# Transposing by two 64-row halves into a pair of neighbouring PSUM banks, in a two-layer decoder trunk

## The chip, the cores and the metric

The kernel runs on one core of one Trainium2 chip. The metric is the device time of one execution in microseconds. Three executions of the kernel before took 1024.15, 1024.07 and 1023.37 us; the median is 1024.07.

The core has several engines that run their own instruction queues side by side and wait for each other by semaphores: PE (TensorE) multiplies matrices, ACT (ScalarE) applies functions and copies, DVE (VectorE) does elementwise arithmetic, POOL (GpSimd) does a little here, and SP (SyncE) issues the DMAs that bring the weights. PE's results land in PSUM, which the kernel uses as 8 banks of 128 partitions by 512 f32; ACT and DVE read them from there.

## The reference

Two layers of a decoder block on 256 tokens of width 1024, in f32:

```python
def hybrid_layer(h, ...):
    h = h + 0.5 * swiglu(rms_norm(h, ffn1_norm), ffn1_w_gate, ffn1_w_up, ffn1_w_down)
    u = rms_norm(h, mix_norm)
    proj = u @ w_in
    # 8 heads of stick-breaking attention (width 512) and 4 heads of latent attention
    # (width 512); each group normalised, concatenated, one output projection
    h = h + mixed @ w_out
    h = h + 0.5 * swiglu(rms_norm(h, ffn2_norm), ffn2_w_gate, ffn2_w_up, ffn2_w_down)
    gate = jax.nn.sigmoid(rms_norm(h, ple_norm) @ w_ple_gate)
    h = h + gate * (p_i @ w_ple_proj)
    return h

def swiglu(x, w_gate, w_up, w_down):
    return (jax.nn.silu(x @ w_gate) * (x @ w_up)) @ w_down
```

After the two layers stands a last `rms_norm`. The hidden width of the FFNs is 2816. Every matrix product sums over the axis that must lie on the 128 partitions, so activations that come out with tokens on the partitions are transposed before the next product.

## The kernel before

**Tiling.** The 256 tokens are two halves t = 0 and 1 of 128. `h` holds the residual stream with tokens on the partitions, 1024 columns for each t. An operand of a matrix product is held transposed, in 8 chunks c of 128 features by 256 tokens, and as two f32r parts, high and low (`x..h` and `x..l`). `mm3` computes a product in three passes: high by high, high by low, low by high (lines 217, 218 and 219 of the profile, in any order of the parts). A pass of 512 columns is one PE instruction.

**Weights.** `Unit.load` fetches 128 × 1024 f32 into `raw` (6 buffers). ACT rounds it to `wh` (L132), DVE subtracts to get `wl` (L133). There are 6 buffers of each. The down projections of the second and third FFN blocks use a seven-product scheme (`Seven`, L168 to L174).

**Transpositions.** PE transposes 128 × 128 tiles by a product with an identity (`ident`, in `c_sb`) into a PSUM bank. There are four kinds. `turn_h` (L328) transposes `h` between stages, four chunks at a time, so two banks for one token half; the tiles are named `xt_a` (FFN1 to mixer), `xt_mix` (mixer to FFN2), `xt_b` (FFN2 to the embedding stage) and `xt_e` (that stage to the next layer). After it, `split` brings each 128 × 128 tile to the next operand: ACT copies it times a gain to the high part (L262), DVE takes the low part from tile and high part (L263). `Gates.add` (L445) transposes the product `pr` of gate and up, four tiles for one t, into a tile `ft`. `turned` (L735) transposes the normalised attention outputs into `yt`. `mla_turn` (L813) transposes the softmax numerators into `pt`.

**PSUM.** One pool `ps` of 8 banks with one tag, so any tile takes the next bank that comes free. A tile that finds none waits until the readers of the oldest are done.

**Order.** The kernel is written once in program order; a scheduler then lists the instructions of each engine by when it thinks their operands are ready, keeping the manual order constraints set by `after`. Work that should come a little later than it becomes possible is put in by `soon(us, f)`: `f` is emitted when PE has been given so many more microseconds of products by the kernel's own count (`tick`: 0.68 for an `mm3` of 512 columns, 0.36 for 256 or fewer). `flush` emits what is left. `residual`, called when a token half's down projection is complete, adds to `h` (L354), asks for the two `turn_h` at 1.2 and 1.9 and then sums squares for the norm (`junk`, L298). `lagging` runs the last chunks of a down projection for t = 0 ahead of those for t = 1, so that t = 0's transposition and splits run beside t = 1's products; the first products of the next stage on t = 0 then run beside those of t = 1.

Of the kernel before, what the change touches and what calls it, by code (L numbers as in the profile page):

```python
# [17 lines left out]
P = 128  # L18
# [27 lines left out]
def trunk(ctx: ExitStack, tc: tile.TileContext, xT, xr, pT, w, gains, fgain, consts, out):  # L46
# [9 lines left out]
    ps = pool("ps", 8, space=PSUM)  # L56

    def bank(name):
        return ps.tile([P, 512], F32, tag="A", name=name)

# [196 lines left out]
    def split(x, src, c, gcol, name, ts=slice(0, T)):  # L257

        xh, xl = x
        g = g_sb[:, gcol : gcol + 1]  # L260
        return (
            nc.scalar.activation(xh[:, c, ts], src, AF.Copy, scale=g),  # L262
            nc.vector.scalar_tensor_tensor(xl[:, c, ts], src, g, xh[:, c, ts].bitcast(F32), op0=ALU.mult, op1=ALU.subtract),  # L263
        )
# [57 lines left out]
    def turn_h(x, t, n, gcol, name):  # L322

        a = bank(f"xt{t}{n}_{name}")
        behind = newest_mm[0]
        for j in range(4):
            c = 4 * n + j
            after(nc.tensor.transpose(a[:, j * P : (j + 1) * P], h[:, t, c * P : (c + 1) * P], ident), behind)  # L328
# [21 lines left out]
    def residual(x, n, d, t, scale, tag, gcol, wait=(1.2, 1.9)):  # L350

        for f in range(2):
            c = half(f)
            nc.vector.scalar_tensor_tensor(h[:, t, c], d[t][f], scale, h[:, t, c], op0=ALU.mult, op1=ALU.add)  # L354
# [30 lines left out]
    class Gates:  # L385
# [19 lines left out]
        def sums(self, i):  # L405
# [6 lines left out]
            s1, s2, s3, s4 = (two[k // 2][:, k % 2].rearrange("p (a b) -> p a b", a=2) for k in range(4))  # L412
# [23 lines left out]
        def add(self, i, t, pr, more):  # L436
# [4 lines left out]
            def go():  # L441
                a = bank(f"ft_{self.tag}_{i}{t}")[:, : n * P]
                behind = newest_mm[0]
                for j in range(n):
                    after(nc.tensor.transpose(a[:, j * P : (j + 1) * P], pr[:, j * P : (j + 1) * P], ident), behind)  # L445
                a = a.rearrange("p (a b) -> p a b", a=n)

                ks = slice(2 if i in SEVEN and t else 0, n)
                fh, fl = both(f, slice(None), ks, slice(t * P, (t + 1) * P))
                nc.scalar.activation(fh, a[:, ks], AF.Copy)  # L450
                nc.vector.tensor_tensor(fl, a[:, ks], fh.bitcast(F32), ALU.subtract)
                self.turned[i, t] = a
                if i in SEVEN and t:
                    self.sums(i)

            soon(1.3 + 0.9 * t + more, go)
# [8 lines left out]
    def ffn(x, n, tag, gcol, between=None, feed=None):  # L465
        gates = Gates(tag)

        def gated(i, t, g, u, m=512):
            s = flat("w0", f"s_{tag}_{i}{t}")[:, :m]
            silu = nc.scalar.activation(s, g, AF.Silu, scale=n.col(t))  # L470

            def rest(more=0.0):
                pr = flat("w1", f"pr_{tag}_{i}{t}")[:, :m]
                nc.vector.scalar_tensor_tensor(pr, u, n.col(t), s, op0=ALU.mult, op1=ALU.mult)
                gates.add(i, t, pr, more)
# [3 lines left out]
        for i in range(NBLK):  # L479
# [4 lines left out]
            if last:  # L484
# [3 lines left out]
                for t in range(2):  # L488
                    silu, rest = gated(i, t, g[t][:, 0:T], g[t][:, T : 2 * T], T)
                    rest()  # L490
# [14 lines left out]
            else:  # L505
# [8 lines left out]
                if i == 1 and feed:  # L514
                    load_consts()
                    exp = newest[0]
                    for t in range(2):
                        silu, r = gated(0, t, first[0][t], first[1][t])
                        after(silu, exp)
                        r(4.5)  # L520
                rests = [gated(i, t, g[t], u[t])[1] for t in range(2)]
# [3 lines left out]
            for r in rests:  # L525
                r()
# [18 lines left out]
        p.update((i, bank(f"p{i}_{tag}")) for i in (1, 5, 6, 7))  # L545
# [27 lines left out]
    def mix(x, n, L, g0):  # L573
# [18 lines left out]
        def sb_scores(hp):  # L592

            st[hp] = zs = [bank(f"z{L}_{hp}_{e}") for e in range(2)]
# [44 lines left out]
        va = [bank(f"v{L}_{t}") for t in range(2)]  # L639
# [18 lines left out]
        uv = wide([Unit(4, again=u) for u in uv])  # L658
        tok_mm(va[1], uv, x, 1)
# [17 lines left out]
        ov = [bank(f"ov{L}_{t}") for t in range(2)]  # L677
# [50 lines left out]
        def turned(o, c0, gcol, name, parts=(0, 1)):  # L728

            for i in parts:  # L730
                a = pair(f"yt{i}_{name}")
                for j in range(2):
                    c = 2 * i + j
                    for t in range(2):
                        nc.tensor.transpose(a[:, j, t * P : (t + 1) * P], o[t][:, c * P : (c + 1) * P], ident)  # L735
                for j in range(2):
                    c = 2 * i + j
                    split(y, a[:, j], c0 + c, gcol + c, name)
# [28 lines left out]
        for i in range(2):  # L767
# [4 lines left out]
            nc.vector.tensor_tensor(kn[:, 2 * i : 2 * i + 2], a, bc(rkv, 2), ALU.mult)  # L772
        ckvT = column(rkv, f"kv{L}")
# [33 lines left out]
        def mla_turn(hp):  # L807
            ex = st["p", hp]
            st["t", hp] = pt = wt("w2", f"pt{L}{hp}", 2, W)
# [281 lines left out]
```

## Time and profile before

| what | before |
|---|---|
| median of three executions | 1024.07 us |
| profiled execution | 1024.05 us |
| its span | 1022.1 us |
| granted TensorE clock | 0.997 |
| DVE busy | 713.2 us, of which wl (L133) 381.8 |
| ACT busy | 603.8 us, of which wh (L132) 332.3 |
| SP's loads of raw | 338 of 512 KB, 16 of 256 KB |

The span runs from the first to the last instruction of one profiled execution; the execution's own time lies 1.95 us above it. A line of the order of time reads: start in us, duration in us, engine, source line, operation, what it writes and reads, shape, number of instructions merged, and where the engine had been idle, for how long and what released it. PEld is the load of stationary operands, which overlaps the products. PE's matmuls are pipelined, so a duration is longer than the distance to the next start, and the distance is what a matmul costs. A row of a group of instructions (`x16 | 5.3, 365 | ...`) gives the number, busy time in all, mean duration in ns and the idle time before. Where durations of one line are listed, they are the least, the median and the greatest.

### The profile page before, as it was taken

What the parts mean: (1) busy time and instruction counts of PE and PEld (TensorE: products, weight loads), DVE (VectorE), ACT (ScalarE), POOL (GpSimd) and SP (SyncE); (2) the same over time, 40 slices, a digit from 0 to 9 for tenths busy, and PEclk for the clock granted to TensorE, in tenths of its full rate; (3) what the DMA queues carried; (4) which work ended last, traced back from release to release, by engine and by line L of the source; (5) the groups of instructions that cost most, each with busy time, mean ns of one, the idle gap of its engine ahead of it and who ended that gap; (6) DMA issues with size and microseconds to landing.
All of it is one profiled execution on the core that took longest, in us unless ns stands there. A gap on an engine that the chain in (4) does not pass through costs nothing.

```text
span 1022.1 us, 13726 instructions
## 1 busy us (share of the span) xinstructions
PE 1010.7 (99%) x5130; PEld 854.9 (84%) x5130; DVE 713.2 (70%) x991; ACT 603.8 (59%) x918; POOL 11.3 (1%) x13
## 2 busy tenths in 40 slices
PE   9999999999999999999999999999999999999996
PEld 8788888899888888888888888889998888888885
DVE  5766579766776665788765656888676756657975
ACT  5755465667565554565764545557766745546664
POOL 0000000100100000000000000001010000000000
PEclk9999999999999999999999999999999999999998
DMA  8865546664246555366565555486623465553651
GB/s 281 317 232 189 180 135 222 216 208 157 83 143 207 186 185 186 123 208 235 183 210 184 185 185 165 145 265 206 207 85 124 154 215 186 186 187 132 220 173 42
DMA packets 53490, 187.39 MB, mean 183 GB/s; under 512 B 6064, under 2 KB 6192, under 8 KB 53424
## 3 DMA queue, kind: packets, MB, share of 16 engines
q1 hardware_dynamic: 52992, 185.95, 54.1%
q8 instruction: 40, 0.66, 0.3%
q10 hardware_dynamic: 432, 0.57, 0.2%
q14 instruction: 26, 0.21, 0.1%
HBM read 185.45 MB, written 1.05 MB: 182 GB/s over the span
## 4 chain that ended last, share of the span: by engine, by line
PE 93%; ACT 3%; DMA 2%; DVE 1%; issue 1%; SPq 0%; DVEq 0%; ACTq 0%
PE g_b L219 4%; PE g_b L217 4%; PE g_b L218 4%; PE g_a L219 4%; PE g_a L217 4%; PE g_a L218 4%; PE u_b L218 4%; PE u_b L217 4%; PE u_b L219 4%; PE u_a L218 3%; PE u_a L219 3%; PE u_a L217 3%; PE d_b L217 3%; PE d_b L219 3%; PE d_b L218 3%; PE d_a L219 3%
## 5 line engine op out<-in xcount | busy, mean ns | idle before, releaser
L133 DVE TENSOR_TENSOR wl<-raw,wh 128x1024 fp32r<-128x1024 f32 (+1 forms) x322 | 381.8, 1195 | 203.6 <-ACT wh L132 199.3
L132 ACT ACTIVATE wh<-raw 128x1024 fp32r<-128x1024 f32 (+1 forms) x322 | 332.3, 1039 | 239.7 <-PE u_b L219 50.2
L173 ACT ACTIVATE wh<-raw 128x1024 fp32r<-128x1024 f32 x56 | 59.5, 1062 | 48.5 <-PE d_b L219 13.3
L174 DVE TENSOR_TENSOR wl<-raw,wh 128x1024 fp32r<-128x1024 f32 x56 | 67.4, 1220 | 18.5 <-ACT wh L173 17.4
L217 PE MATMUL d_a<-wh,fh_a 128*128 128x512 f32 x128 | 50.3, 394 | 0.0
L217 PE MATMUL d_b<-wh,fh_b 128*128 128x512 f32 x128 | 50.3, 393 | 0.0
L218 PE MATMUL d_a<-wl,fh_a 128*128 128x512 f32 x128 | 50.0, 391 | 0.0
L218 PE MATMUL d_b<-wl,fh_b 128*128 128x512 f32 x128 | 50.0, 391 | 0.0
L219 PE MATMUL d_b<-wh,fl_b 128*128 128x512 f32 x128 | 49.9, 389 | 0.0
L219 PE MATMUL d_a<-wh,fl_a 128*128 128x512 f32 x128 | 49.9, 389 | 0.0
L168 DVE TENSOR_TENSOR raw<-raw,raw 128x1024 f32<-128x1024 f32 x32 | 38.7, 1219 | 8.1 <-DMA raw<-in_w 8.0
L217 PE MATMUL g_b<-wh,x_mix0h 128*128 128x512 f32 x96 | 38.4, 400 | 0.0
L217 PE MATMUL g_b<-wh,x_mix1h 128*128 128x512 f32 x96 | 38.4, 400 | 0.0
L217 PE MATMUL g_a<-wh,x0h 128*128 128x512 f32 x96 | 38.1, 399 | 0.3 <-ACT x0h L262 0.3
L217 PE MATMUL g_a<-wh,xe0h 128*128 128x512 f32 x96 | 38.4, 400 | 0.0
L219 PE MATMUL g_a<-wh,xe0l 128*128 128x512 f32 x96 | 37.6, 391 | 0.0
L219 PE MATMUL g_b<-wh,x_mix1l 128*128 128x512 f32 x96 | 37.5, 390 | 0.0
L219 PE MATMUL g_b<-wh,x_mix0l 128*128 128x512 f32 x96 | 37.5, 390 | 0.0
L218 PE MATMUL g_b<-wl,x_mix0h 128*128 128x512 f32 x96 | 37.4, 390 | 0.0
L218 PE MATMUL g_b<-wl,x_mix1h 128*128 128x512 f32 x96 | 37.4, 390 | 0.0
L218 PE MATMUL g_a<-wl,xe0h 128*128 128x512 f32 x96 | 37.4, 390 | 0.0
L219 PE MATMUL g_a<-wh,x0l 128*128 128x512 f32 x96 | 37.3, 390 | 0.0
(450 smaller groups left out, 2504.0 us busy)
## 6 DMA issues: line engine op xcount, KB each, us to landing
raw<-in_w SPq DMA_DIRECT2D x338, 512.0 KB, 4.1
raw<-in_w SPq DMA_DIRECT2D x16, 256.0 KB, 4.7
xin<-in_xT SPq DMA_DIRECT2D x4, 256.0 KB, 5.2
h<-in_xr SPq DMA_DIRECT2D x2, 512.0 KB, 9.3
p<-in_pT SPq DMA_DIRECT2D x2, 256.0 KB, 6.4
fg<-in_fgain SPq DMA_DIRECT2D x1, 512.0 KB, 4.5
out_h<-hg SPq DMA_DIRECT2D x2, 256.0 KB, 2.3
out_h<-hg ACTq DMA_DIRECT2D x2, 256.0 KB, 2.7
```

Of the source, the lines that this page charges most:

```text
L132: nc.scalar.activation(wh[:, a], r[:, a], AF.Copy),
L133: nc.vector.tensor_tensor(wl[:, a], r[:, a], wh[:, a].bitcast(F32), ALU.subtract),
L168: nc.vector.tensor_tensor(self.raw[o], self.raw[a], self.raw[b], op)
L173: newest_wh[0] = nc.scalar.activation(wh, r, AF.Copy)
L174: nc.vector.tensor_tensor(wl, r, wh.bitcast(F32), ALU.subtract)
L217: nc.tensor.matmul(o, ah, bh, start=start, stop=False, **kw)
L218: nc.tensor.matmul(o, ah, bl, start=False, stop=False, **kw)
L219: newest_mm[0] = nc.tensor.matmul(o, al, bh, start=False, stop=stop, **kw)
```

## The change

Every transposition of 128 × 128 becomes two of 64 rows: rows 0 to 63 and rows 64 to 127 of the source, each against the matching 64 × 64 block of the identity. The first gives 128 × 64 in one bank, the second 128 × 64 in the neighbouring one, at the same place in the bank. A PSUM tile for it spans two banks (`banks2`), and there is one such pair; the other six banks stay single. The new helper `turn` issues the transpositions of a whole turn, with the two halves in alternation:

```diff
+    def turn(o, parts, behind=None):
+        for i, src in enumerate(parts):
+            for e in range(2):
+                r = slice(64 * e, 64 * e + 64)
+                m = nc.tensor.transpose(o[:, e, 64 * i : 64 * i + 64], src[r], ident[r, r])
+                if behind is not None:
+                    after(m, behind)
+                behind = m
-    ps = pool("ps", 8, space=PSUM)
+    ps = pool("ps", 6, space=PSUM)
+    ps2 = pool("ps2", 1, space=PSUM)
-    def turn_h(x, t, n, gcol, name):
-        a = bank(f"xt{t}{n}_{name}")
-        behind = newest_mm[0]
-        for j in range(4):
-            c = 4 * n + j
-            after(nc.tensor.transpose(a[:, j * P : (j + 1) * P], h[:, t, c * P : (c + 1) * P], ident), behind)
-        for j in range(4):
-            c = 4 * n + j
-            split(x, a[:, j * P : (j + 1) * P], c, gcol + c, name, slice(t * P, (t + 1) * P))
+    def turn_h(x, t, gcol, name):
+        a = banks2(f"xt{t}_{name}")
+        turn(a, [h[:, t, c * P : (c + 1) * P] for c in range(KC)], newest_mm[0])
+        for c in range(KC):
+            split(x, a[:, :, c * 64 : (c + 1) * 64], c, gcol + c, name, slice(t * P, (t + 1) * P))
-    def residual(x, n, d, t, scale, tag, gcol, wait=(1.2, 1.9)):
+    def residual(x, n, d, t, scale, tag, gcol, wait=1.9):
-            soon(wait[f], lambda f=f: turn_h(x, t, f, gcol, tag))
+        soon(wait, lambda: turn_h(x, t, gcol, tag))
...
-            soon(1.3 + 0.9 * t + more, go)
+                o = banks2(f"ft_{self.tag}_{i}")
+                turn(o, [pr[:, j * P : (j + 1) * P] for j in range(n) for pr in prs], newest_mm[0])
+            soon(1.9 + more, go)
```

So `turn_h` now does all eight chunks of one token half in one turn, at 1.9; `Gates.add` does both token halves in one turn; `mla_turn` takes two heads in one turn. `split`, the copies after `ft`, `sums` and the copies to `pt` read each tile from both banks. Other uses are moved to the pair: the first two z of the stick-breaking scores, their outputs `ov`, the latent group's outputs `om`, and the products `p5` and `p7` of the seven-product scheme. The second bank of v is taken later.

```diff
-            st[hp] = zs = [bank(f"z{L}_{hp}_{e}") for e in range(2)]
+            z = None if hp else banks2(f"z{L}_{hp}")
+            st[hp] = zs = [bank(f"z{L}_{hp}_{e}") if hp else z[:, e] for e in range(2)]
...
-        ov = [bank(f"ov{L}_{t}") for t in range(2)]
+        ov = banks2(f"ov{L}")
...
+            a = banks2(f"yt_{name}")
+            turn(a, [o[t][:, c * P : (c + 1) * P] for c in range(4) for t in range(2)])
+            for c in range(4):
+                for t in range(2):
+                    split(y, a[:, c, t], c0 + c, gcol + c, name, slice(t * P, (t + 1) * P))
...
-        soon(2.6, turn)
-        soon(4.0, values)
+        soon(2.0, lambda: mla_turn(0))
+        soon(3.6, lambda: mla_turn(1))
+        soon(4.9, values)
...
-            soon(4.0 + 0.7 * i, lambda i=i: turned(on, 4, g0 + G_MLA, f"mla{L}", (i,)))
+        soon(4.3, lambda: turned(on, 4, g0 + G_MLA, f"mla{L}"))
...
-                        soon(4.4 if f == 0 else 2.8, lambda t=t, f=f: turn_h(nx, t, f, gcol, f"e{L}"))
+                    elif f:
+                        soon(2.8, lambda t=t: turn_h(nx, t, gcol, f"e{L}"))
```

The transposition of the stick-breaking outputs (`turned(on, 0, ...)`) is moved ahead of the latent group's values `vm` in program order; `mla_turn(0)` copies by DVE and `mla_turn(1)` by ACT, where both were copied by ACT; the first products with `w_out` run t by t.

What this makes of the instruction order, at the two places that matter most. First PE, where FFN1 of the first layer hands over to the mixer (d_a is FFN1's down projection, for t = 1 at this place, and xt_a the transposed h of t = 0). Before:

```order
L219 MATMUL d_a_1164<-wh_0_0_76_1540,fl_a_4_1059 128x512
L328 MATMUL xt_a_1608<-c_sb,h 128x128 x4
L217 MATMUL d_a_1163<-wh_1_0_77_1552,fh_a_4_1058 128x512
L218 MATMUL d_a_1163<-wl_1_0_77_1553,fh_a_4_1058 128x512
L219 MATMUL d_a_1163<-wh_1_0_77_1552,fl_a_4_1059 128x512
L328 MATMUL xt_a_1624<-c_sb,h 128x128 x4
L217 MATMUL d_a_1164<-wh_1_0_77_1552,fh_a_4_1058 128x512
```

And PE at the same place with the change:

```order
L222 MATMUL d_a_1201<-wh_1_0_77_1592,fh_a_4_1091 128x512
L223 MATMUL d_a_1201<-wl_1_0_77_1593,fh_a_4_1091 128x512
L224 MATMUL d_a_1201<-wh_1_0_77_1592,fl_a_4_1092 128x512
L335 MATMUL xt_a_1651<-c_sb,h 128x64 x16
L222 MATMUL d_a_1202<-wh_1_0_77_1592,fh_a_4_1091 128x512
```

Two groups of four transpositions with a product between them have become one group of sixteen half transpositions, three matmuls later, into one tile. The turn for t = 1 follows 38 matmuls later: 15 of d_a and 23 of v's 24, which need the splits of t = 0 one chunk after the other.

Second DVE at that handover, from the first split of t = 0 on (x_a0l is the low part of the mixer's input, wl the low part of the weights, h the residual add, hr_a small pieces of the norm). Before:

```order
L133 TENSOR_TENSOR wl_1_0_83_1734<-raw_1_0_83_1735,wh_1_0_83_1733 128x1024
L263 SCALAR_TENSOR_TENSOR x_a0l<-xt_a_1608,g_sb,x_a0h 128x128
L263 SCALAR_TENSOR_TENSOR x_a0l<-xt_a_1624,g_sb,x_a0h 128x128
L354 SCALAR_TENSOR_TENSOR h<-d_a_1163,h 128x512
L263 SCALAR_TENSOR_TENSOR x_a0l<-xt_a_1608,g_sb,x_a0h 128x128
L354 SCALAR_TENSOR_TENSOR h<-d_a_1164,h 128x512
L263 SCALAR_TENSOR_TENSOR x_a0l<-xt_a_1608,g_sb,x_a0h 128x128
L263 SCALAR_TENSOR_TENSOR x_a0l<-xt_a_1624,g_sb,x_a0h 128x128
L133 TENSOR_TENSOR wl_0_0_84_1757<-raw_0_0_84_1758,wh_0_0_84_1756 128x1024
L263 SCALAR_TENSOR_TENSOR x_a0l<-xt_a_1624,g_sb,x_a0h 128x128
```

And with the change, from the second h on, where four of the eight splits have still to come, up to the first split of t = 1:

```order
L368 SCALAR_TENSOR_TENSOR h<-d_a_1202,h 128x512
L138 TENSOR_TENSOR wl_0_0_84_1810<-raw_0_0_84_1811,wh_0_0_84_1809 128x1024
L270 SCALAR_TENSOR_TENSOR x_a0l<-xt_a_1651,g_sb,x_a0h 128x128
L309 TENSOR_TENSOR hr_a_1579<-hss_a_1578 128x1
L138 TENSOR_TENSOR wl_1_0_85_1828<-raw_1_0_85_1829,wh_1_0_85_1827 128x1024
L270 SCALAR_TENSOR_TENSOR x_a0l<-xt_a_1651,g_sb,x_a0h 128x128
L289 TENSOR_SCALAR hr_a_1579<-hr_a_1579 128x1
L138 TENSOR_TENSOR wl_0_0_86_1871<-raw_0_0_86_1872,wh_0_0_86_1870 128x1024
L270 SCALAR_TENSOR_TENSOR x_a0l<-xt_a_1651,g_sb,x_a0h 128x128
L283 TENSOR_TENSOR hr_a_1579<-hr_a_1579,y_a_1707 128x1
L138 TENSOR_TENSOR wl_1_0_87_1889<-raw_1_0_87_1890,wh_1_0_87_1888 128x1024
L270 SCALAR_TENSOR_TENSOR x_a0l<-xt_a_1651,g_sb,x_a0h 128x128
```

Each of the last splits of t = 0 now stands behind a further wl, and another wl and split follow these rows; before, the eighth split stood behind the second wl and the splits of t = 1 came next.

More of the change, by code (lines that the diff above doesn't have):

```diff
@@ L411, in sums @@
             two = [wt(f"w{2 + k}", f"sum{k}_{self.tag}_{i}") for k in range(2)]
-            s1, s2, s3, s4 = (two[k // 2][:, k % 2].rearrange("p (a b) -> p a b", a=2) for k in range(4))
+            s1, s2, s3, s4 = (two[k // 2][:, k % 2].rearrange("p (a e b) -> p a e b", a=2, e=2) for k in range(4))
             nc.scalar.copy(s3, b[:, lo])
@@ L434, in seven, with add @@
             return of
-        def add(self, i, t, pr, more):
+        def add(self, i, prs, more):
             f = self.block(i)
@@ L441, in go @@
             def go():
[L442 to L453, printed above, removed]
+                o = banks2(f"ft_{self.tag}_{i}")
+                turn(o, [pr[:, j * P : (j + 1) * P] for j in range(n) for pr in prs], newest_mm[0])
+                a = o[:, :, : n * P].rearrange("p e (c t b) -> p t c e b", c=n, t=2)
+                for t in range(2):
+                    ks = slice(2 if i in SEVEN and t else 0, n)
+                    fh, fl = (q[:, ks, t * P : (t + 1) * P].rearrange("p c (e b) -> p c e b", e=2) for q in f)
+                    nc.scalar.activation(fh, a[:, t, ks], AF.Copy)
+                    nc.vector.tensor_tensor(fl, a[:, t, ks], fh.bitcast(F32), ALU.subtract)
+                    self.turned[i, t] = a[:, t]
+                if i in SEVEN:
                     self.sums(i)
-            soon(1.3 + 0.9 * t + more, go)
+            soon(1.9 + more, go)
     def seven_mm(banks, x_of, ops, first, last):
@@ L515, in ffn @@
                     load_consts()
[L516 to L521, printed above, removed]
+                    gated(0, *first, behind=newest[0])[1](4.5)
+                rest = gated(i, g, u)[1]
                 for k in range(KC):
@@ L524, in ffn @@
                         tok_mm(u[t], wu, x, t, (k,))
-            for r in rests:
-                r()
+            rest()
         d = four(f"d_{tag}")
@@ L544, in ffn @@
         p = {2: d[0][0], 3: d[0][1], 4: d[1][0]}
-        p.update((i, bank(f"p{i}_{tag}")) for i in (1, 5, 6, 7))
+        two = banks2(f"p_{tag}")
+        p.update(((1, bank(f"p1_{tag}")), (5, two[:, 0]), (6, bank(f"p6_{tag}")), (7, two[:, 1])))
         own = (1, 5, 6, 7)
@@ L676, in mix @@
         sb_scores(3)
-        ov = [bank(f"ov{L}_{t}") for t in range(2)]
+        ov = banks2(f"ov{L}")
+        ov = [ov[:, t] for t in range(2)]
         sb_values(0)
@@ L726, in token_norm, with turned @@
             return out
[L728 to L738, printed above, removed]
+        def turned(o, c0, gcol, name):
+            a = banks2(f"yt_{name}")
+            turn(a, [o[t][:, c * P : (c + 1) * P] for c in range(4) for t in range(2)])
+            a = a.rearrange("p e (c t b) -> p c t e b", c=4, t=2)
+            for c in range(4):
+                for t in range(2):
+                    split(y, a[:, c, t], c0 + c, gcol + c, name, slice(t * P, (t + 1) * P))
         sb_values(2)
@@ L832, in mix @@
         om = []
-        def turn():
-            mla_turn(0)
-            mla_turn(1)
         def values():
-            om.extend(bank(f"om{L}_{i}") for i in range(2))
+            o = banks2(f"om{L}")
+            om.extend(o[:, t] for t in range(2))
             mla_values(0)
```

53 lines of the change are left out of this document (30 added, 23 removed).

## The prediction

> **What bounds the kernel now.** I read the busy shares first, then the chain of work that ended last.
>
> ```profile
> PE 1010.7 (99%) x5130; PEld 854.9 (84%) x5130; DVE 713.2 (70%) x991; ACT 603.8 (59%) x918; POOL 11.3 (1%) x13
> ...
> PE 93%; ACT 3%; DMA 2%; DVE 1%; issue 1%; SPq 0%; DVEq 0%; ACTq 0%
> ```
>
> PE sets the time: it is busy 99% of the span, and 93% of the chain is PE. So a change pays in two ways only: by the time that PE itself spends, or by holes that it opens or closes on PE. The shares of 70% and 59% for DVE and ACT are averages over very unlike stages. The table by windows, for the stretch in which the first FFN hands over to the mixer, says more:
>
> ```profile
> 184.00:199.00 15.00, 15.00 (x83) 12.74 (x82) 13.13 (x36) 14.21 (x35) 0.00 (x0) 1.00 0.54 184
> ```
>
> The columns are the window, its length, then PE, PEld, DVE and ACT busy. Here DVE works 13.13 of 15 us and ACT 14.21, beside a PE without a hole. The handover is balanced to within a microsecond or two on three engines. The granted clock is 1.00, so it plays no part.
>
> **Term 1: the transpositions on PE.** What they cost now is in the order of time on PE:
>
> ```profile
> 46.12 0.39 PE L219 MATMUL u_a<-wh,x0l 128*128 128x512 f32 x1
> 46.35 0.60 PE L445 MATMUL ft_a<-c_sb,pr_a 128*128 128x128 f32 x4
> 46.70 0.47 PE L217 MATMUL u_a<-wh,x0h 128*128 128x512 f32 x1
> 47.02 0.39 PE L218 MATMUL u_a<-wl,x0h 128*128 128x512 f32 x1
> ```
>
> A 512-column matmul takes 46.35 − 46.12 = 0.23 us, 0.227 where many follow each other. From 46.12 to 47.02 there are two of them and four transpositions: 0.90 − 0.46 = 0.44, so 0.11 us for each transposition, and nothing for going in or out. Their number:
>
> ```profile
> L445 PE MATMUL ft_a<-c_sb,pr_a x88: 270/272/273, 46.3 to 638.8; 128*128 128x128 f32 x88
> L445 PE MATMUL ft_b<-c_sb,pr_b x88: 270/272/273, 321.2 to 929.4; 128*128 128x128 f32 x88
> L328 PE MATMUL xt_a<-c_sb,h x32: 270/272/273, 185.5 to 696.9; 128*128 128x128 f32 x32
> L328 PE MATMUL xt_mix<-c_sb,h x32: 270/272/273, 292.2 to 803.6; 128*128 128x128 f32 x32
> L328 PE MATMUL xt_b<-c_sb,h x32: 270/272/273, 476.0 to 987.4; 128*128 128x128 f32 x32
> L328 PE MATMUL xt_e<-c_sb,h x16: 270/272/273, 494.8 to 514.3; 128*128 128x128 f32 x16
> L735 PE MATMUL yt_sb<-c_sb,on_sb x16: 271/272/273, 263.1 to 767.5; 128*128 128x128 f32 x16
> L735 PE MATMUL yt_mla<-c_sb,on_mla x16: 270/272/273, 283.1 to 788.1; 128*128 128x128 f32 x16
> L813 PE MATMUL pt<-c_sb,ex x24: 270/272/328, 272.0 to 777.0; 128*128 128x128 f32 x24
> ```
>
> That is 344, or 344 × 0.11 = 37.8 us: all that halving could touch. Afterwards there are 344 pairs in 46 turns: 38 turns of 8 pairs (20 ft, 14 xt, 4 yt), 4 of 4 pairs (the last, narrow ft block) and 4 of 6 (pt). The nearest rows for 64-row work are the scores of the stick-breaking heads, which are already two heads in the two halves of the rows:
>
> ```profile
> 217.81 0.28 PE L218 MATMUL k<-x_a0l,wh 128*128 128x256 f32 x1
> 217.93 0.28 PE L219 MATMUL k<-x_a0h,wl 128*128 128x256 f32 x1
> 218.14 0.70 PE L598 MATMUL z<-sbq,sbk 64*128 64x256 f32 x4
> 218.67 0.39 PE L600 MATMUL z<-sbq,sbk 64*128 64x128 f32 x4
> 218.99 0.50 PE L602 MATMUL z<-c_r 128*128 128x256 f32 x2
> 219.33 0.28 PE L217 MATMUL k<-x_a0h,wh 128*128 128x256 f32 x1
> ```
>
> Four f32 passes of 256 columns fit in 218.67 − 218.14 = 0.53 us. One after the other, at 0.11 for 128 columns, they would take 0.88; two at a time, 0.44. So the halves do run together. But the change of form is not free. A pass of 256 columns of the ordinary kind takes 0.12 (217.81 to 217.93), so the real work of L602's two passes begins at 219.33 − 0.24 = 219.09, while L600's four passes of 128 columns (two at a time, 0.22) end at 218.67 + 0.22 = 218.89: 0.20 us is lost going out. Going in, L219 ends its columns at 218.05, and the first 256-column pass must begin at 218.67 − 0.43 = 218.24: 0.19 lost, of which about 0.1 is a load of weights in the open. A transposition's load is shorter: the one pt matmul whose load stood open took 328 ns where the others take 272, so 0.056 open. I take 0.15 in and 0.20 out, **0.35 a turn**.
>
> A pair has 64 columns to stream in each half, half of 0.11: I take 0.055, which is also the 0.056 of one load. A full turn is 8 × 0.055 + 0.35 = 0.79 against 0.88 before: −0.09, times 38 = −3.4. A turn of four pairs is 0.57 against 0.44: +0.13, times 4 = +0.5. Six pairs: 0.68 against 0.66, +0.1 in all. **Term 1 is −2.8 us**. The bounds: if nothing is lost at the change of form, half of 37.8 goes, −18.9. If a pair takes the full 0.11 of a transposition, because two loads share one path, nothing is halved and 46 × 0.35 = +16 is paid.
>
> The Trainium skill, "TensorE: Matmul & The Clock Gate", section "LDWEIGHTS (loading the stationary operand)", holds that a load goes by its columns, P/1.2 ns whatever the rows; for 128 columns that is 107 ns, and by it two loads on one path would make this term +16. The open transposition load of 56 ns speaks against that figure here. The same skill's "TensorEngine Tiling (Array Packing)", "Key Properties", says that changing the tiling mode drains TensorE, and the 0.20 us of the rows above agrees; its "Theoretical Speedup" table, up to twice for a dimension of 64, would be −18.9 and leaves that drain out.
>
> **Term 2: one pair where there were two banks.** The diff gives every turn the same pair of banks, with one buffer. Before, a token half's transposition took two banks, and the next half found others free. Now the second half's turn must wait until the eighth split of the first has read the pair. Each split is an ACT copy and then a DVE subtraction, and on one tile ACT's next copy waits for DVE's last:
>
> ```profile
> L262 ACT ACTIVATE x_b1h<-xt_b,g_sb 128x128 fp32r<-128x128 f32 x16 | 5.3, 365 | 1.6 <-DVE x_b1l L263 1.4
> ```
>
> Of 1.6 us that ACT idled before these copies, 1.4 were ended by the subtraction. Two tiles alternated so far; now there is one. The prices, from the handover to the mixer:
>
> ```profile
> 185.46 0.60 PE L328 MATMUL xt_a<-c_sb,h 128*128 128x128 f32 x4
> ...
> 188.01 0.34 DVE L263 SCALAR_TENSOR_TENSOR x_a0l<-xt_a,g_sb,x_a0h 128x128 fp32r<-128x128 f32 x1
> ...
> 189.01 1.23 DVE L133 TENSOR_TENSOR wl<-raw,wh 128x1024 fp32r<-128x1024 f32 x1
> 190.16 0.60 DVE L263 SCALAR_TENSOR_TENSOR x_a0l<-xt_a,g_sb,x_a0h 128x128 fp32r<-128x128 f32 x2
> 190.68 0.68 DVE L354 SCALAR_TENSOR_TENSOR h<-d_a,h 128x512 f32<-128x512 f32 x1
> ...
> 194.06 0.34 DVE L263 SCALAR_TENSOR_TENSOR x_a0l<-xt_a,g_sb,x_a0h 128x128 fp32r<-128x128 f32 x1
> 194.32 0.15 DVE L302 TENSOR_TENSOR hr_a<-hss_a 128x1 f32<-128x1 f32 x1
> ```
>
> ```profile
> 187.23 0.37 ACT L262 ACTIVATE x_a0h<-xt_a,g_sb 128x128 fp32r<-128x128 f32 x1
> 187.92 1.06 ACT L132 ACTIVATE wh<-raw 128x1024 fp32r<-128x1024 f32 x1 [0.33 <-PE d_a L219]
> 188.89 0.60 ACT L262 ACTIVATE x_a0h<-xt_a,g_sb 128x128 fp32r<-128x128 f32 x2
> ...
> 511.54 1.28 ACT L100 ACT_TABLE_LOAD   x1
> ```
>
> From one start to the next a wl takes 1.15 (189.01 to 190.16), a split 0.26, a wh 0.97; a link of the chain is 0.37 + 0.34 = 0.71.
>
> Handover **xt_a** (twice). In the new DVE order six wl stand between the first and the last split of t = 0; only one stood among the first seven before. PE has 38 matmuls, 38 × 0.227 = 8.6 us, between the two turns. The first turn starts three matmuls after the first group of before (185.46 + 0.68 = 186.1) and ends at 186.9, so PE could arrive at 195.5. DVE begins its first split at 188.0, as before. Its queue to the last split is 6 × 1.15 + 8 × 0.26 + 2 × 0.68 and some smalls at under 0.15: about 10.9, so 198.9 at the earliest, a hole of 3.4. Stepping both queues by hand with ACT's seven copies and wh between them gives 11.4, so 199.4: 3.9. Behind the waiting turn stand the last matmul of v and all of q and k, which need t = 1's splits, one ACT copy and one subtraction later: 0.6 after that. **+4.5 each, +9.0**. Bounds 3.4 and 6.2 (links fully in series).
>
> Handover **xt_mix** (twice): 26 matmuls of cover, 5.9 us. First copy and wait 0.65, a wl and an h still ahead on DVE, and the stepped chain of 8 links with one wl, two h and two sums of squares is 7.25: about 8.4, a hole of 2.5. Then t = 1's eight splits with four wl between them, 6.6 us, feed a PE that needs them in 8 × 0.68 = 5.4: I take 0.8. **+3.3 each, +6.6**, bounds 0.4 and 6.
>
> Handover **xt_e** (once): 32 matmuls, 7.3 us; the stepped chain holds two wh, a sigmoid and the table load of 1.28: 9.7, and 0.6 after it. **+3.0**, bounds 0 and 6. Handover **xt_b** (twice): 10.4 us of cover for a chain of some 9.4: **+0.5 each, +1.0**, bounds 0 and 6 for both. In **MLA** yt_sb's chain, pt of two heads, pt of the next and om take the pair in turn:
>
> ```profile
> 273.14 0.31 PEld L813 LDWEIGHTS pt<-c_sb,ex 128*128 128x128 f32 x3 [0.26 <-ACT ex L805]
> ```
>
> PE waits here already for the exponentials, and pt's copies now stand between: **+0.7 each, +1.4**, bounds 0 and 3 for both. In the gate loops a turn comes three mm3, 2.0 us, after the last u, and its product is ready about 1 us after: no hole. The pair is free long before; were the product 1 us late, 20 turns would show it, +20. The turned y now takes eight splits of 128 columns for each group where four of 256 stood: at 0.71 a link some 1.5 us more of ACT and DVE each time, in series with the pair; yt_sb's part of that is in the 0.7 above, yt_mla's is ahead of xt_mix's first turn, whose delay stands in the 8.4. SP's and POOL's instructions keep their sequence, so no load moves past another.
>
> **The sum.** 9.0 + 6.6 + 3.0 + 1.0 + 1.4 = 21.0, less 2.8: +18.2. The profiled execution took 1024.05 us, span 1022.1 and 1.95 around it, and stands at the median of 1024.07. So **1042 us**.
>
> **The rivals.**
> - *A pair costs as much as a transposition.* For it: loads are listed at 138 to 140 ns and one path may feed both halves. Against it: the open load of 56 ns. Term 1 becomes +16: 1024 + 16 + 21 = 1061.
> - *The change of form is hidden or small*, holes as forecast. For it: a turn is more densely queued than the scores. Against it: the 0.19 and 0.20 us were lost with loads queued there too. 1024 − 18.9 + 21 = 1026.
> - *The second turn finds the pair free* (the other side). The place is the turn of t = 1 in xt_a. If the eight splits end within PE's 8.6 us, under 1.0 us a link from the first, no hole opens there, nor at the better covered places: 1024 − 2.8 = 1021, 1005 with the form free as well. It decides by where DVE takes its six wl; against it stands that 10.9 us of work is queued on DVE up to the last split, in that order.
> - *The change doesn't do what it says*: the pairs run one half after the other; that is the first rival's time.
>
> **How the numbers follow.** Forecast 0.60; a pair at full price 0.14; form free 0.13 (0.03 faster, 0.04 same, 0.06 slower); pair free 0.13 (0.10 faster, 0.03 same). Faster by over 0.2% (about 2 us, what a measurement of this kernel can tell from none) 0.13, within 0.2% 0.07, slower 0.80. With all holes at their low ends (6.8 + 0.8) the forecast's own sum is 1029, with all at the high ends (12.4 + 12 + 6 + 6 + 3) 1061. The range is 1027 to 1061: it leaves out what the form being free, or a pair that is free in time, would bring.
>
> **What would show it.** In the profile of the changed kernel PE's idle time before xt_a, xt_mix and xt_e should name the splits on DVE as releaser, some 4, 2.5 and 2.5 us at each place, and PE's share of the chain should fall by two points. A full turn should add 0.79 us between its neighbours. If turns add 1.2, the first rival holds; if 0.45, the second. No idle time before the t = 1 turns would refute term 2, and with it the sign.

## The result, and the profile after

The changed kernel takes 1047.87 us in the median (1047.51 to 1048.62), beside 1023.94 us for the kernel before on the same chip: a ratio of 1.0241, 95% interval 1.0228 to 1.0253. It is slower by 24 us; 18 were forecast. The profiled execution took 1047.51 us, its span is 1045.6 us and the granted clock 0.997, as before.

The page of the changed kernel, busy shares and the chain that ended last:

```profile
PE 1023.9 (98%) x5474; PEld 839.6 (80%) x5474; DVE 721.9 (69%) x1011; ACT 614.1 (59%) x930; POOL 7.4 (1%) x13
...
PE 91%; ACT 4%; DVE 3%; issue 1%; DMA 0%; SPq 0%; ACTq 0%
```

PE has 344 more instructions, as the halving says. PE's share of the chain fell from 93% to 91%. 93% of 1022.1 and 91% of 1045.6 are both about 951 us, so the loss lies outside PE's own work. To see where it lies, compare the first start and the last of one group in each layer, first before, then after (duration least, median and greatest in ns; first and last start):

```profile
L217 PE MATMUL v<-wh,x_a0h x16: 389/389/477, 190.5 to 228.3; 128*128 128x512 f32 x16
...
L217 PE MATMUL wo<-wh,y0h x32: 389/389/481, 269.2 to 296.5; 128*128 128x512 f32 x32
...
L217 PE MATMUL g_b<-wh,x_mix0h x96: 389/389/481, 297.2 to 421.8; 128*128 128x512 f32 x96
...
L217 PE MATMUL g_a<-wh,xe0h x96: 389/389/481, 510.6 to 634.8; 128*128 128x512 f32 x96
```

```profile
L222 PE MATMUL v<-wh,x_a0h x16: 389/389/499, 188.8 to 230.9; 128*128 128x512 f32 x16
...
L222 PE MATMUL wo<-wh,y0h x32: 387/393/504, 273.1 to 301.5; 128*128 128x512 f32 x32
...
L222 PE MATMUL g_b<-wh,x_mix0h x96: 389/389/500, 303.3 to 430.8; 128*128 128x512 f32 x96
...
L222 PE MATMUL g_a<-wh,xe0h x96: 389/389/501, 519.1 to 647.4; 128*128 128x512 f32 x96
```

The changed kernel is 1.7 us ahead when v begins and 2.6 behind when v's second half ends: 4.3 went at the handover to the mixer. At the first wo it is 3.9 behind, so 1.3 more, and the order of time puts all of that into the scores z. At the first g_b it is 6.1 behind (2.2 in wo), at the last 9.0 (2.9 at the handover to FFN2), at the first g_a of the next layer 8.5, at its last 12.6 (4.1 at that handover). The second layer repeats it: 4.4, 1.3, 2.2 and 2.9. Of the 1.7 us at the start, 0.9 is a wait for an early weight at 40 us, which the profiled executions of some of these kernels have, before among them, and others don't.

What happens at the handover to the mixer is in the order of time on PE of the changed kernel (in brackets how long PE had nothing to do, and what ended it):

```profile
191.72 0.49 PE L224 MATMUL v<-wh,x_a0l 128*128 128x512 f32 x1
192.90 0.50 PE L222 MATMUL v<-wh,x_a0h 128*128 128x512 f32 x1 [0.69 <-ACT x_a0h L269]
193.24 0.39 PE L223 MATMUL v<-wl,x_a0h 128*128 128x512 f32 x1
193.47 0.40 PE L224 MATMUL v<-wh,x_a0l 128*128 128x512 f32 x1
194.10 0.50 PE L222 MATMUL v<-wh,x_a0h 128*128 128x512 f32 x1 [0.24 <-ACT x_a0h L269]
...
196.20 0.49 PE L224 MATMUL v<-wh,x_a0l 128*128 128x512 f32 x1 [0.33 <-DVE x_a0l L270]
196.65 0.50 PE L222 MATMUL v<-wh,x_a0h 128*128 128x512 f32 x1
196.99 0.40 PE L223 MATMUL v<-wl,x_a0h 128*128 128x512 f32 x1
197.96 0.72 PE L335 MATMUL xt_a<-c_sb,h 64*128 64x64 f32 x16 [0.57 <-issue]
198.61 0.50 PE L224 MATMUL v<-wh,x_a0l 128*128 128x512 f32 x1
```

Three passes of v should take 0.68; here a chunk takes 1.2 (192.90 to 194.10). PE goes through v at the pace at which the splits of t = 0 arrive, one chunk after the other. The turn of t = 1 starts at 197.96, with 0.57 us of idle time before it. So the splits are late, and most of the holes stand before v, not before the turn. On DVE the eight splits run from the first to the last of these:

```profile
186.38 0.35 DVE L270 SCALAR_TENSOR_TENSOR x_a0l<-xt_a,g_sb,x_a0h 128x128 fp32r<-128x128 f32 x1
...
197.52 0.34 DVE L270 SCALAR_TENSOR_TENSOR x_a0l<-xt_a,g_sb,x_a0h 128x128 fp32r<-128x128 f32 x1
```

That is 11.5 us (to 197.86, from 186.38); 11.4 had been stepped by hand. The turn of t = 1 starts 0.1 us after the last split ends, as one that needs the pair must. The profile names no releaser here, and in the second layer a small DVE instruction that follows the last split.

In wo the same shows on a smaller scale. PE's order and, below it, DVE's:

```profile
290.28 0.39 PE L224 MATMUL wo<-wh,y0l 128*128 128x512 f32 x1
290.70 0.50 PE L222 MATMUL wo<-wh,y0h 128*128 128x512 f32 x1
291.04 0.39 PE L223 MATMUL wo<-wl,y0h 128*128 128x512 f32 x1
...
291.97 0.75 PE L224 MATMUL wo<-wh,y0l 128*128 128x512 f32 x2
...
290.43 1.23 DVE L138 TENSOR_TENSOR wl<-raw,wh 128x1024 fp32r<-128x1024 f32 x1 [1.23 <-ACT wh L137]
291.57 0.34 DVE L270 SCALAR_TENSOR_TENSOR y0l<-yt_mla,g_sb,y0h 128x128 fp32r<-128x128 f32 x1
```

The twelve passes of a chunk of y, 2.7 us without holes, take 3.4 (290.70 to 294.13). After every second split DVE waits for a weight's high part and makes a wl before it takes the next split.

A full turn itself, in the gate loop, where nothing waits:

```profile
52.35 0.39 PE L224 MATMUL g_a<-wh,x0l 128*128 128x512 f32 x1
52.67 0.71 PE L335 MATMUL ft_a<-c_sb,pr_a 64*128 64x64 f32 x16
53.31 0.50 PE L222 MATMUL g_a<-wh,x0h 128*128 128x512 f32 x1
53.65 0.40 PE L223 MATMUL g_a<-wl,x0h 128*128 128x512 f32 x1
```

From L224 to L223 are 1.30 us with two passes of 0.227 in it, so the turn costs 0.85. The same reckoning gives 0.60 for a turn of four pairs and 0.72 to 0.75 for one of six: 0.062 a pair and 0.35 for going in and out. Two groups of four transpositions before cost 0.89, at 0.447 each, close to the 0.44 of the group that the prediction had picked.

### The profile page after: what moved, and what is told of

Read it like the earlier page. It is cut to its first block, busy times and chain, and to the rows that moved or that the text cites. A ratio compares the mean times of both kernels' runs of the same rounds, so it can differ in the third digit from the quotient of the medians.

```text
span 1045.6 us, 14441 instructions
## 1 busy us (share of the span) xinstructions
PE 1023.9 (98%) x5474; PEld 839.6 (80%) x5474; DVE 721.9 (69%) x1011; ACT 614.1 (59%) x930; POOL 7.4 (1%) x13
## 4 chain that ended last, share of the span: by engine, by line
PE 91%; ACT 4%; DVE 3%; issue 1%; DMA 0%; SPq 0%; ACTq 0%
PE g_b L222 4%; PE g_a L222 4%; PE g_b L224 4%; PE g_a L224 4%; PE g_a L223 4%; PE g_b L223 4%; PE u_a L222 3%; PE u_b L222 3%; PE u_a L223 3%; PE u_b L224 3%; PE u_b L223 3%; PE u_a L224 3%; PE d_b L222 3%; PE d_b L223 3%; PE d_b L224 3%; PE d_a L222 3%
## 5 line engine op out<-in xcount | busy, mean ns | idle before, releaser
L223 PE MATMUL d_a<-wl,fh_a 128*128 128x512 f32 x128 | 49.8, 389 | 0.0
L223 PE MATMUL d_b<-wl,fh_b 128*128 128x512 f32 x128 | 49.8, 389 | 0.0
L224 PE MATMUL d_a<-wh,fl_a 128*128 128x512 f32 x128 | 49.8, 389 | 0.0
L224 PE MATMUL d_b<-wh,fl_b 128*128 128x512 f32 x128 | 49.8, 389 | 0.0
L224 PE MATMUL g_a<-wh,xe0l 128*128 128x512 f32 x96 | 37.9, 395 | 0.8 <-DVE xe0l L270 0.8
L224 PE MATMUL g_b<-wh,x_mix0l 128*128 128x512 f32 x96 | 37.8, 394 | 0.2 <-DVE x_mix0l L270 0.2
L224 PE MATMUL g_b<-wh,x_mix1l 128*128 128x512 f32 x96 | 37.8, 394 | 0.2 <-DVE x_mix1l L270 0.2
L223 PE MATMUL g_b<-wl,x_mix0h 128*128 128x512 f32 x96 | 37.5, 391 | 0.0
L223 PE MATMUL g_a<-wl,xe0h 128*128 128x512 f32 x96 | 37.5, 390 | 0.0
L223 PE MATMUL g_b<-wl,x_mix1h 128*128 128x512 f32 x96 | 37.5, 390 | 0.0
L223 PE MATMUL g_a<-wl,x0h 128*128 128x512 f32 x96 | 37.2, 390 | 0.0
```

What stands on the lines that cost most here:

```text
L223: nc.tensor.matmul(o, ah, bl, start=False, stop=False, **kw)
L224: newest_mm[0] = nc.tensor.matmul(o, al, bh, start=False, stop=stop, **kw)
```

## The experiments

All ratios are to the kernel before, run on the same chip; the changed kernel stands at 1.0241.

**Is it the 64-row form?** The same turns and the same pair, with 128 rows again:

```diff
+        flat_o = o.rearrange("p a b -> p (a b)")
...
-            for e in range(2):
-                r = slice(64 * e, 64 * e + 64)
-                m = nc.tensor.transpose(o[:, e, 64 * i : 64 * i + 64], src[r], ident[r, r])
...
+            m = nc.tensor.transpose(flat_o[:, P * i : P * i + P], src, ident)
```

> The changed kernel with every transposition of 128 rows again, into the same pair of banks, in the same turns, with the same waits. Theory (the 64-row form itself is worth next to nothing; the loss comes from one pair for all turns): a full turn goes from 0.855 to 8 x 0.11 = 0.88 us (38 of them, +0.8), a turn of four from 0.607 to 0.44 (4, -0.7), a turn of six from 0.725 to 0.66 (4, -0.3): about -0.2 in all, so 1047.7 us, and the holes before v, wo, g_b and g_a stay as they are. Rival (reading a tile out of two banks in 64-column pieces is what makes the splits late): the holes go and it takes 1024 to 1035 us.

1046.91 us, ratio 1.0234 (1.0219 to 1.0249). A full turn takes 0.88 in this run, as expected. The halving is worth nothing that can be measured, and reading a tile out of two banks is not what makes the splits late. What is left is the pair and the order that comes with it.

**Do two halves run at once?** The order inside a turn alone:

```diff
-        for i, src in enumerate(parts):
-            for e in range(2):
+        for e in range(2):
+            for i, src in enumerate(parts):
```

> The changed kernel with the order inside a turn alone changed: all transpositions of rows 0 to 63 first, then all of rows 64 to 127, instead of in alternation. If the alternation lets two run at once, a full turn goes from 0.855 to about 0.36 + 16 x 0.06 = 1.3 us (38 turns, +17), those of four and six pairs by 0.25 and 0.37 (+2.5), less where a turn stands before a hole: 1062 to 1067 us. If the halves of a turn ran one after the other already, or overlap in any order, 1047 to 1048.5 us.

1061.16 us, ratio 1.0375 (1.0361 to 1.0389), 13.7 us above the changed kernel and a little less than expected. The turn in the gate loop of this kernel, and the narrow turn of four pairs:

```profile
53.99 0.39 PE L224 MATMUL g_a<-wh,x0l 128*128 128x512 f32 x1
54.31 1.01 PE L335 MATMUL ft_a<-c_sb,pr_a 64*128 64x64 f32 x16
55.25 0.50 PE L222 MATMUL g_a<-wh,x0h 128*128 128x512 f32 x1
55.59 0.40 PE L223 MATMUL g_a<-wl,x0h 128*128 128x512 f32 x1
...
134.90 0.39 PE L224 MATMUL d_a<-wh,fl_a 128*128 128x512 f32 x1
135.22 0.47 PE L335 MATMUL ft_a<-c_sb,pr_a 64*128 64x64 f32 x8
135.62 0.50 PE L222 MATMUL d_a<-wh,fh_a 128*128 128x512 f32 x1
135.96 0.40 PE L223 MATMUL d_a<-wl,fh_a 128*128 128x512 f32 x1
```

1.60 − 0.45 = 1.15 instead of 0.85 for the full turn. But four and four cost 1.06 − 0.45 = 0.61, against 0.60 in alternation. The single starts in the traces say why. In one half of the rows, after the first, a transposition follows another about every 0.062 us, in either order of issue. In alternation the two of a pair start 0.003 us apart. With four behind four each of the second four starts 0.013 to 0.015 us after its partner, and with eight behind eight only four of the second half run beside the first half. So the halves do overlap, and the alternation matters where the groups are longer than four. The change does what it says.

**Which tiles?** First h in single banks as before (`turn_one` is the old `turn_h`, with the old waits 1.2 and 1.9), for both token halves:

```diff
-        soon(wait, lambda: turn_h(x, t, gcol, tag))
+        if t in (0, 1):
+            for f in range(2):
+                soon((1.2, 1.9)[f], lambda f=f: turn_one(x, t, f, gcol, tag))
+        else:
+            soon(wait, lambda: turn_h(x, t, gcol, tag))
...
+                    elif t in (0, 1):
+                        soon(4.4 if f == 0 else 2.8, lambda t=t, f=f: turn_one(nx, t, f, gcol, f"e{L}"))
```

> The changed kernel, but h is transposed between stages as before: 128 rows, four chunks at a time, into two single banks. ft, yt, pt and the rest keep the pair. Theory (eight splits in series on one tile make the handovers late): the holes in v and q (4.35 us, twice), g_b (2.95, twice) and g_a of the second layer (4.1) go, -18.7, and 14 turns cost 0.05 more: about 1030 us. Rival (six single banks are too few, whatever the turn does): at least half of the 18.7 stays, 1038 us or more, with waits of PE for the readers of single banks.

1032.61 us, ratio 1.0094 (1.0079 to 1.0109): 15 us of the 24, less than the 18.7 expected, since g_b still waits 1.1 us for splits in each layer. The list of PE's waits names none for a reader of a single bank, so six are enough for it. Then the attention outputs alone, with the old form of `turned` and its waits (4.0 and 4.7):

> The changed kernel, but the normalised attention outputs are transposed as before, 128 rows into two single banks, with four splits of 256 columns for each group instead of eight of 128. Theory (the eight splits of yt_mla in series on the pair starve the products with w_out): the holes in wo, 2.2 us in each layer, go, and xt_mix finds the pair free earlier: -4.4 to -6, 1042 to 1043.5 us. Rival (the holes in wo come from the weights or from the new order of wo's products): 1047.9 us, no change.

1042.81 us, ratio 1.0192 (1.0176 to 1.0207): 5 us, as expected, in wo and in the turn of xt_mix behind it. Then the first scores:

```diff
-            z = None if hp else banks2(f"z{L}_{hp}")
-            st[hp] = zs = [bank(f"z{L}_{hp}_{e}") if hp else z[:, e] for e in range(2)]
+            st[hp] = zs = [bank(f"z{L}_{hp}_{e}") for e in range(2)]
```

> The changed kernel, but the scores z of the first two stick-breaking heads lie in two single banks. Theory (PE writes the second head's half of the shared tile only after ACT has read the first head's, 0.93 us each layer): the stage from z to ov loses 0.9 to 1.3 us in each layer, -1.9 to -2.6, 1045.3 to 1046 us. Rival (the single banks that it takes are missed elsewhere): 1048 us or more.

1047.59 us, ratio 1.0241 (1.0224 to 1.0258): nothing, a miss. The hole had stood in the changed kernel before the tail of the second head, whose half of the shared tile PE may write only after ACT has read the first's:

```profile
233.03 0.39 PE L616 MATMUL z<-c_r 128*128 128x256 f32 x1
234.08 0.45 PE L637 MATMUL z<-nh,c_r 128*128 128x384 f32 x1 [0.66 <-ACT a L640]
```

That wait is gone in this run, but z still loses 1.2 us in each layer: another wait stands in its place, with the third pair of heads:

```profile
232.94 1.31 PE L611 MATMUL z<-sbq,sbk 64*128 64x256 f32 x3
233.77 0.49 PE L613 MATMUL z<-sbq,sbk 64*128 64x128 f32 x2
234.09 0.38 PE L611 MATMUL z<-sbq,sbk 64*128 64x256 f32 x1
234.30 0.38 PE L613 MATMUL z<-sbq,sbk 64*128 64x128 f32 x2
```

The passes of the two heads no longer alternate: three passes, two, then the last one and two more. The second head's first pass waits for ACT, the last reader of the bank that its tile gets (there are six), so its work follows the first head's instead of running beside it.

**Which half of h?** If both token halves share one pair, either may be the one that suffers. So each alone was taken out of it:

```diff
-        soon(wait, lambda: turn_h(x, t, gcol, tag))
+        if t in (1,):
+            for f in range(2):
+                soon((1.2, 1.9)[f], lambda f=f: turn_one(x, t, f, gcol, tag))
+        else:
+            soon(wait, lambda: turn_h(x, t, gcol, tag))
...
```

> The changed kernel, but h of the second token half (t = 1) alone is transposed as before, into two single banks; t = 0 keeps the pair. Nothing waits for the pair between the two halves any more. Theory A (the turn of t = 1 waits for a pair that t = 0 still holds): most of the holes at the three handovers go, -12 or more, 1036 us or less. Theory B (the eight splits of t = 0 in series on one tile, with weights' low parts put between them on DVE, come too late for the first products of the next stage): the holes in v, g_b and g_a ahead of the t = 1 turn stay, and only the wait of that turn (0.64 and 0.31 us) and something behind it go: 1042 to 1047 us.

> The changed kernel, but h of the first token half (t = 0) alone is transposed as before, into two single banks; t = 1 keeps the pair, which is free for it. Theory B (the splits of t = 0 in series on one tile are late): the holes in v (3.5 of 4.35 us in each layer), and most of those in g_b and g_a go, -11 to -15: 1033 to 1037 us, a little above the kernel with both halves in single banks (1032.6). Theory A (the pair is held) says the same of this one, since t = 1 finds its pair free; the two part in the run with t = 1 alone.

1035.68 us for t = 1 (1.0130, 1.0113 to 1.0147) and 1035.80 for t = 0 (1.0126, 1.0111 to 1.0141): each gives back 11 to 12 of the 15 us, but not in the same places. The loss by stage in the traces of these runs, from the starts of v, wo, g_b and g_a against the kernel before, in us. ("t = 1 out" and "t = 0 out" are these two runs, "h out" the run with both halves in single banks, "y out" the one with the attention outputs.)

| stage | changed | t = 1 out | t = 0 out | h out | y out |
|---|---|---|---|---|---|
| v, q and k, both layers | 8.7 | 0.7 | 0.1 | 0.0 | 8.7 |
| wo, both | 4.4 | 4.4 | 4.5 | 4.5 | 0.4 |
| end of wo to last g_b, both | 5.8 | 2.7 | 5.5 | 3.0 | 4.3 |
| last g_b to next layer's last g_a, once | 3.6 | 2.6 | 0.2 | −0.2 | 4.8 |

At the mixer either half alone gives back nearly all, so theory B falls there: with t = 1 in single banks the splits of t = 0 are still in series on one tile, and the loss goes all the same. At the next layer's FFN1 theory B is the better one: with t = 1 out the waits before g_a stay (1.0 and 0.7 us in the list), and with t = 0 out they go. At FFN2 neither theory is enough. There 3.0 us stay with all of h out, and in the run with the attention outputs out as well (below) nothing stays: h's splits share that loss with those of y ahead of them.

How it goes at the mixer, PE's order in the run with t = 1 out shows:

```profile
192.76 0.28 PE L224 MATMUL q<-x_a0h,wl 128*128 128x256 f32 x1
193.06 0.50 PE L222 MATMUL v<-wh,x_a0h 128*128 128x512 f32 x1
193.40 0.39 PE L223 MATMUL v<-wl,x_a0h 128*128 128x512 f32 x1
193.62 0.28 PE L222 MATMUL q<-x_a0h,wh 128*128 128x256 f32 x1
193.74 0.28 PE L222 MATMUL k<-x_a0h,wh 128*128 128x256 f32 x1
193.86 0.28 PE L223 MATMUL k<-x_a0l,wh 128*128 128x256 f32 x1
193.98 0.40 PE L224 MATMUL v<-wh,x_a0l 128*128 128x512 f32 x1
```

v still advances at the pace of the splits, a chunk in 1.9 us at the slowest. But t = 1 is transposed meanwhile, so q and k, which need both halves of a chunk, stand between v's passes. (With t = 0 out, v isn't late at all: its chunks start 0.68 to 0.81 us apart, but for the two between which the turn of t = 1 stands.) In the changed kernel q and k can't fill in: t = 1 isn't there before the last split of t = 0 has been taken. Sixteen splits through one pair are one chain, and at the mixer PE has nothing that doesn't depend on its next link.

**Is it where DVE takes the weights?** One constraint more: weights for q and k after the last split of t = 0.

```diff
+            last_split[t] = split(x, a[:, :, c * 64 : (c + 1) * 64], c, gcol + c, name, slice(t * P, (t + 1) * P))
...
+        fence[:] = last_split[0]
         q0, k0 = pair(f"q0{L}"), pair(f"k0{L}")
...
+        fence[:] = None, None
         keep(sbq, 2, q1, 0.125)
```

> The changed kernel with one thing moved: the high and low parts of the weights of q and k (five or more of each) may be made on ACT and DVE only after the eighth split of t = 0, in the handover to the mixer. Tiles, turns and the pair stay. Theory C (it is where DVE takes the weights' low parts, between the splits, that makes v late): eight links at 0.75 and two h end about 3.5 us earlier, the holes in v go; q then waits for its weights, some 1 to 2 us. 2 to 3 us less in each layer: 1042 to 1044 us. Rival D (DVE has that work to do before PE can go on in any case): what v gains q loses, 1047 to 1048.5 us.

1047.28 us, ratio 1.0237 (1.0222 to 1.0252). That is rival D's time: v's holes go, and q and k wait instead, as the list of what PE waited for in this run says (us in all, times, longest):

```profile
PE k L224 <- DVE wl L138: 1.2, 2, 0.6
PE q L223 <- DVE x_a0l L270: 1.1, 1, 1.1
PE q L223 <- DVE x_a1l L270: 1.1, 1, 1.1
```

The exchange is not quite even. In the traces the stage of v, q and k loses 6.7 us in both layers instead of 8.7; the early weight wait, which the profiled execution has, hides about half of that in its time. Theory C had expected 2 to 3 us in each layer. That neither order serves because the splits of t = 1 wait behind those of t = 0 in both is the likely reason; no run separates it.

**Is it the number of links?** On top of `x1_rows128`, in whose tiles both token halves of a chunk lie next to each other, the attention outputs by 256 columns:

```diff
-            for c in range(4):
-                for t in range(2):
-                    split(y, a[:, c, t], c0 + c, gcol + c, name, slice(t * P, (t + 1) * P))
+            for c in range(4):
+                split(y, a[:, c * T : (c + 1) * T], c0 + c, gcol + c, name)
```

> The kernel with 128-row transpositions into the pair (x1_rows128), and one thing more: the attention outputs are split by 256 columns, both token halves in one instruction, four for each group instead of eight; tile, turn and pair stay. Theory (the number of splits in series on the pair starves the products with w_out): four links of about 0.95 us take the place of eight of 0.71, 1.9 us less, and most of the holes in wo (1.7 to 2.2 us in each layer) go: -3 to -4.4 against x1_rows128, 1042.5 to 1044 us. Rival (the pair itself, one tile for the whole group, is what is late): 1046 to 1047 us.

1043.77 us, ratio 1.0208 (1.0192 to 1.0224), by the ratios 2.7 us below `x1_rows128`, a little short of the 3 to 4.4. The pair is the same, and wo loses 0.2 us in both layers instead of 3.5. So the pair itself is not what starves wo. That the number of splits is, this comparison doesn't show, because the holes of `x1_rows128` stand elsewhere:

```profile
291.02 1.29 PE L334 MATMUL yt_mla<-c_sb,on_mla 128*128 128x128 f32 x8 [0.77 <-DVE on_mla L738]
292.76 0.50 PE L222 MATMUL wo<-wh,y0h 128*128 128x512 f32 x1 [0.46 <-ACT y0h L269]
293.10 0.39 PE L223 MATMUL wo<-wl,y0h 128*128 128x512 f32 x1
```

Its turn waits for the normalised outputs, and the first product behind it for the first split. The seven splits that follow come 0.79 us apart, all eight in series on the pair with no wl between them, and PE doesn't wait for one. In the run with four splits the normalised outputs also come earlier: no weight's parts stand ahead of them on ACT and DVE, where here one of each does. The changed kernel, with a wl after every second split, does lose at the pace of its splits. So wo's loss goes with the splits and the order of ACT and DVE around them, and the share of the mere number stays open.

**The parts together.** h, the attention outputs and the first scores in single banks:

> The changed kernel with h, the attention outputs and the first scores in single banks as before; the pair is left to ft, ov, pt, om and two products. If the parts add up, -15.3 and -5 with what they share (xt_mix behind yt_mla) counted once: 1027 to 1029 us. What stays is the second bank that z waits for with six single banks, about 1.3 us in each layer. Rival (yt and xt together want more than six single banks): above 1032 us.

1025.21 us, ratio 1.0019 (1.0010 to 1.0029), better than the 1027 that was thought the least. By stage, z still loses 2.4 us in both layers and wo 0.5, the rest nothing; FFN2's 5.8 are gone. And with the third scores in the pair, ov in single banks:

```diff
+            z = banks2(f"z{L}_{hp}") if hp == 2 else None
+            st[hp] = zs = [z[:, e] if hp == 2 else bank(f"z{L}_{hp}_{e}") for e in range(2)]
...
-        ov = banks2(f"ov{L}")
-        ov = [ov[:, t] for t in range(2)]
+        ov = [bank(f"ov{L}_{t}") for t in range(2)]
```

> The changed kernel with h and the attention outputs in single banks as before (x7), and with the scores of the third pair of heads in the pair of banks and ov in two single banks, so that z finds its second bank. The hole of 1.2 us in z of each layer should go: 1022.5 to 1023.5 us, no longer slower than the kernel before; 1025 or more if ov in single banks takes a bank that another tile waits for.

1022.61 us, ratio 0.9999 (0.9990 to 1.0008). All of the loss is gone, and in the list of PE's waits in this run one line is left, a wait at the very start. z has no hole here, though the third pair of heads shares the pair. The 64-row form stays in ft, pt and nothing else, and brings nothing that can be measured. No run was faster than the kernel before.

## Why the prediction was right, point by point

Both terms and the sign held, and the sum was 6 us too low. The stages by the shifts above, which hold the turns' own share of a few hundredths each:

| step of the prediction | forecast, us | measured, us |
|---|---|---|
| transpositions on PE (price by number, in all stages) | −2.8 | −1.0 |
| handover xt_a, both layers | +9.0 | +8.7 |
| handover xt_mix, both | +6.6 | +5.8 |
| handover xt_e | +3.0 | +4.1 |
| handover xt_b, both | +1.0 | −0.5 |
| MLA up to the first wo, both | +1.4 | 0 |
| wo behind yt_mla, both | in the above | +4.4 |
| scores z, both | none | +2.6 |

The rows from xt_a on add up to 25.1, and with the 1.7 us by which the changed kernel is ahead at v that is the 23.4 by which the spans differ.

- **Term 1** was mis-sized. A pair takes 0.062, not 0.055, and going in and out 0.35, as forecast, so a full turn is 0.846 against 0.894: 38 × −0.048 = −1.8, plus 0.5 for the narrow turns of four and 0.3 for those of six. Both prices came from rows of another operation and were right within 14%. The first rival, a pair at full price, is refuted by the 0.062; where the halves mostly run one behind the other, as in the run with eight and eight, the time comes to the 1061 forecast for it. The form-free rival is refuted by the 0.35.
- The Trainium skill, "TensorE: Matmul & The Clock Gate", section "LDWEIGHTS (loading the stationary operand)", would give each of these loads of 128 columns an estimated 107 ns. In the traces loads in one half of the rows start 0.062 us apart, so that figure doesn't hold for them; nor did it decide the sum. Nor does the prediction's +16 follow from it: two such loads one behind the other would make a pair 0.21 us, not 0.11. The Trainium skill, "TensorEngine Tiling (Array Packing)", section "Key Properties", says that a change of mode drains TensorE, and the 0.35 agrees with that.
- **Term 2** held in size: the first three lines of it were forecast at 18.6 and measured at 18.6, though single lines are off by up to 1.1 and that they cancel is luck. At xt_a the two runs that take h's halves out of the pair one by one show the mechanism, and the chain ends where it was stepped to (11.5 and 11.4 us). At xt_mix the wait for the pair between h's halves is not the whole of it: 3.0 of the 5.8 us stay when all of h is out, and go only when y is out too.
- **The place** was wrong. The prediction expected PE to stand idle before the t = 1 turns, some 4, 2.5 and 2.5 us, and called their absence a refutation. PE idles 0.6 us before each such turn of xt_a and not at all before those of xt_mix and xt_e. It stands ahead of them, before v, g_b and g_a, since these need the same late splits and come first in PE's order. At xt_a the 38 matmuls counted as cover could not run ahead: 23 of them are v's. The price is the same, since the turn of t = 1 still comes at the end of the chain.
- **The step that was wrong** is "yt_mla's is ahead of xt_mix's first turn, whose delay stands in the 8.4". It looked at the pair alone and not at who reads y: wo's products need the eight splits of yt_mla as they come, and lost 2.2 us in each layer. Two runs with four splits in place of eight gave nearly all of that back, one in single banks and one in the pair.
- **What was left out**: two tiles of different heads put into one pair are one tile to the waits. PE's write for one head waits for ACT's read of the other, 0.9 us in each layer. Giving z its banks back moved that hole to the next tile; only the last kernel, which also moved ov, was without it.
- The rival of the other side, the pair free in time, would have needed the chain to end within 8.6 us. It took 11.5.

What stays open: what the chain would cost if ACT's copies did not have to wait for DVE's subtraction on the same tile, and how wo's loss divides between the number of splits and the order around them. This wasn't tried.

## What to carry to other kernels

A faster operation on the bounding engine is worth its gain only if the buffers that it needs are as many as before: here the operation itself came out 1.0 us ahead in all by its prices, and the one pair of banks that it required, with the order that came with it, cost 25. When a buffer becomes single, ask not only who waits to write it but what the bounding engine could still do meanwhile; at the mixer two independent chains let it fill one's gaps from the other, and one chain of twice the length didn't. A sum that comes back can hide that: two runs gave back the same 12 us, in different stages. And price an operation that needs a change of form on PE as a fixed sum for each group plus its own time: a pair gains 0.05 us here, so below about seven pairs the 0.35 us ate the gain whole.

## What the runs showed of the hardware

Two halves of the rows run side by side, but a long run in one half holds the other up. Sixteen half transpositions cost 0.85 us in alternation and 1.15 us as eight and eight; eight of them cost 0.60 and 0.61, as four and four. All of these include the 0.35 us of changing the form. In one half of the rows transpositions of 64 f32 columns start 0.062 us apart, somewhat more than half of the 0.11 for 128 rows and 128 columns. Rows and columns were halved together, so no run here says which of the two sets the price.
